# Value projections of the second mixer: from plain products to blocks of two column groups with sevens

## The chip, the cores and the metric

The kernel runs on one core of one Trainium2 chip. The metric is the device time of one launch in microseconds, as the median of several runs. TensorE multiplies matrices and writes into banks of accumulators, VectorE and ScalarE do elementwise work, SyncE (SP) issues the weight loads. Each engine works through its own queue in order and waits on semaphores for the others.

## The reference

Two layers over 256 positions of width 2048. Each layer adds a mixer and a gated feed-forward stage to the residual stream h. The first layer's mixer is a gated delta rule with a recurrent unit, the second layer's mixer is two kinds of attention, eight heads of 128 each; the change is in the second.

```python
def fox_moba_mixer(hn, w_in, f_bias, w_out):
    fq, fk, fv, ff, mq, mk, mv = split_cols(hn @ w_in, CD_SIZES)
    log_f = jax.nn.log_sigmoid(ff.astype(jnp.float32) + f_bias.astype(jnp.float32)).transpose(0, 2, 1)
    o_c = forgetting_attention(to_heads(fq, FOX_HEADS), to_heads(fk, FOX_HEADS), to_heads(fv, FOX_HEADS), log_f)
    o_d = moba_attention(partial_rotary(to_heads(mq, MOBA_HEADS)), partial_rotary(to_heads(mk, MOBA_HEADS)),
                         to_heads(mv, MOBA_HEADS))
    return jnp.concatenate([from_heads(o_c), from_heads(o_d)], axis=-1) @ w_out

def reference(x, ...):
...
    for layer in range(DEPTH):
        j = layer // 2
        if layer % 2 == 0:
            h = h + gdn_rglru_mixer(rmsnorm(h, ab_norm[j]), ...)
        else:
            h = h + fox_moba_mixer(rmsnorm(h, cd_norm[j]), cd_w_in[j], cd_f_bias[j], cd_w_out[j])
        h = h + swiglu(rmsnorm(h, ffn_norm[layer]), ffn_w_gate[layer], ffn_w_up[layer], ffn_w_down[layer])
    return rmsnorm(h, final_norm)
```

With 256 positions the second kind of attention (moba) has one block, so it is plain causal attention with a partial rotation. The values fv and mv are two products of 256 x 2048 by 2048 x 1024.

## The kernel before

**Precision.** Each matrix product is made of three matmuls of a reduced-precision format: an operand is split into a high part (a cast on ScalarE, L179) and a low part (the difference, on VectorE, L180); high x high, high x low and low x high are summed in one accumulator. The activations X are kept as high and low parts, tokens along the free dimension, 16 feature tiles of 128.

**Loads.** `load` (L166) fetches 512 KB of weights into one of three buffers `raw`; in the feed-forward stages some loads go to four further buffers, `raw4`. `split` makes `whi` (four buffers) and `wlo` (three). One load with its split is called a unit here.

**Products.** There are two ways to hold the operands. `wstat` (L187) keeps the weights stationary and makes queries and keys: 32 matmuls per 128 columns, with X's both parts moving. `xstat` (L280) keeps X stationary and streams weights of 512 columns: per unit two feature tiles, two halves of the tokens and three matmuls each, 12 matmuls of 512 columns; it uses two of the four large accumulators (`acc`). The values are made by `xstat`, one column group of 512 after the other, eight units each (`values`, L1033). The output projections use it too.

**Sevens.** The feed-forward stages use `block` (L409) instead. It makes two column groups and both token halves at once, in four accumulators F, and can do some feature groups (four feature tiles, 512 features) by seven products in place of eight, as Strassen and Winograd do with 2 x 2 blocks. The two operands' sums are made on VectorE: `combine` (L382) makes the four combinations of X of a feature group, `total` (L372) the four sums of weight blocks, each split again into a high part `thi` and a low part `tlo`. Four of the products go to four small accumulators M (the tag `ms`, four banks), three straight into F. When all sevens are done, `ends` (L449) makes from M the four corrections e0 to e3, and the caller adds each to, or subtracts it from, its F. `lead` and `trail` say how many plain units stand before and after the sevens.

**Order of the work.** Attention of each head is a generator (`attend`, L1042) with four steps. `tick` (L156), called after each unit, moves waiting generators on; the forgetting gate (`forget`, L1001) is one too. `need` runs generators until something is done, `finish` runs them all. So small matmuls of attention stand between the large ones of projections. They take their accumulators from the same four small banks. A scheduler of the language then fixes each engine's order of instructions from dependences and priorities; buffers of one tag rotate, and a new tile waits until the last reader of the buffer is done.

**The second mixer** (`mixer1`, L995): values of the first kind, the norm's reciprocal root (`rstd`, whose rows are then spread by `rstd_rows`), the forget gate, eight heads of queries and keys with their attention into `Of`; values of the second kind, eight heads with rotation and attention into `Om`; then the output projection over `Of` and over `Om`. `vv`, `Of` and `Om` are the three buffers of 16 KB per partition of the pool `og`.

Of the kernel before, what the change touches and what calls it, by code (L numbers as in the profile page):

```python
# [11 lines left out]
T = 256  # L12
# [35 lines left out]
def body(tc, A, out):  # L48
# [14 lines left out]
    loads, more = [0], []  # L63

    def phase(mixer):

        st = ExitStack()
        sub = lambda name, bufs: st.enter_context(tc.tile_pool(name=name, bufs=bufs))
        ogp.pool = sub("og" if mixer else "hid", 3 if mixer else 1)
        if not mixer:  # L70

            fp.pool = sub("fp", 1)
        mx.pool = sub("mx" if mixer else "fx", 1)
        more[:] = [] if mixer else [1]
        loads[0] = -12
        return st
# [265 lines left out]
    def rstd_rows():  # L342

        rs = nrm["rs"]
        dg = mx.tile([128, 2, 128], F32, name="dg", tag="t1", bufs=5)
# [36 lines left out]
    def combine(x4):  # L382

        f = mx.tile([128, 4, T], F32, name="cf", tag="T", bufs=3)
        c = mx.tile([128, 4, 2, 128], F32, name="cc4", tag="T", bufs=3)
        r = fp.tile([128, 2, 4, 2, 128], F32R, name="comb", tag="comb", bufs=3)
        V.tensor_tensor(out=f, in0=x4[:, :, 0].bitcast(F32), in1=x4[:, :, 1].bitcast(F32), op=ALU.add)
        a11, a21, a12, a22 = (f[:, 2 * j:2 * j + 2, t * 128:(t + 1) * 128] for j in range(2) for t in range(2))
        for i, (x, y) in enumerate(((a21, a22), (a21, a11), (a22, c[:, 1]), (a12, c[:, 2]))):
            V.tensor_tensor(out=c[:, i], in0=x, in1=y, op=ALU.subtract)  # L390
        S.copy(r[:, 0], c)
        V.tensor_tensor(out=r[:, 1], in0=c, in1=r[:, 0].bitcast(F32), op=ALU.subtract)
        return r
# [15 lines left out]
    def block(src, x, comb, nd, hooks, tail=0, lead=2, trail=None):  # L409
# [50 lines left out]
        for j, (i, u) in enumerate(plain):  # L460
# [91 lines left out]
    def small_proj(src, n):  # L552

        raw = mx.tile([128, NK, n], F32, name="sraw", tag="t1", bufs=5)
# [41 lines left out]
    def mixer0():  # L596
# [101 lines left out]
        def pair_task(pr):  # L698
# [8 lines left out]
            for j, hd in enumerate(hds):  # L707
                qk = qks[hd]
                sq = mx.tile([128, 2, 2, 128], F32, name="sq", tag="t2", bufs=4)
                vg = mx.tile([128, 2, 128], F32, name="vg", tag="t1", bufs=5)  # L710
# [11 lines left out]
                dec = mx.tile([128, 2, 128], F32, name="dec", tag="t1", bufs=5)  # L722
# [46 lines left out]
        def group_task(gr):  # L769
# [7 lines left out]
            Vc = mx.tile([128, 8, 32], F32, name="Vc", tag="t1", bufs=5)  # L777
# [36 lines left out]
            V1 = mx.tile([128, 8, 32], F32, name="V1", tag="t1", bufs=5)  # L814
# [11 lines left out]
            V1 = mx.tile([128, 8, 32], F32, name="V3", tag="t1", bufs=5)  # L826
# [146 lines left out]
        for n in range(8):  # L973
            lw = mx.tile([128, 2, 128], F32, name="lw", tag="t1", bufs=5)
# [20 lines left out]
    def mixer1():  # L995
# [35 lines left out]
        Om = ogp.tile([128, 8, 2, T], F32R, name="Om", tag="og")  # L1031

        def values(i):  # L1033
            for g in range(2):
                Ps = xstat(lambda k: X[:, k], [A["w1x"][2 * i + g, u] for u in range(8)])
                if i == g == 0:
                    rstd()
                    start(forget(), 1)
                for t in range(2):
                    V.tensor_scalar_mul(vv[:, i, t, g * 512:(g + 1) * 512], Ps[t], nrm["rs"][:, t:t + 1])  # L1040

        def attend(i, hd, q, k, O):  # L1042
            if i == 0:

                sel = mx.tile([40, 128], F32R, name="sel", tag="kt", bufs=HB)
# [38 lines left out]
        def qk_head(i, hd):  # L1084
            r = []
            for which in range(2):
                t = scaled(wstat(W[16 * i + 2 * hd + which], True), "qkt", SCALE if which == 0 else 1.0, "vt", HB)
                if i == 1:
                    sw = mx.tile([32, T], F32, name="sw", tag="t1", bufs=5)
# [20 lines left out]
        out_proj(lambda k: Om[:, k], lambda g: [wo[g, 4 + u] for u in range(4)], norm_then(cl["n3"]))  # L1110
# [166 lines left out]
```

## Time and profile before

| what | value |
|---|---|
| runs (3) | 2231.83, 2232.99, 2235.12 us; median 2232.99 |
| profiled execution, device time | 2232.51 us |
| its span in the profile | 2230.7 us |
| granted TensorE clock | 0.999 |
| TensorE busy | 2215.9 us, 99% |
| VectorE busy | 1928.9 us, 86% |
| ScalarE busy | 1278.9 us, 57% |

A page of the profile shows the busy time of each engine, the chain of work that ended last, and groups of instructions by source line with mean duration, idle time ahead and what ended it. PE is TensorE's matmuls, PEld its weight loads, DVE VectorE, ACT ScalarE, SPq the queue of SP. Names like `wlo<-raw,whi` are the program's tiles, output first. Busy time of TensorE overlaps from one matmul to the next; the distance between two starts is the price of one. The second mixer lies between 1128 and 1525 us of the span.

### The profile page before, as it was taken

The numbers are of one execution on the slowest core, as the hardware profiler recorded it, in microseconds if no ns is written. First come the engines' busy times: TensorE is split into PE (matmuls) and PEld (weight loads), VectorE is DVE, ScalarE is ACT, GpSimd is POOL, SyncE is SP. The second block draws the span as 40 slices with busy tenths as digits, with TensorE's granted clock in tenths as the row PEclk, the third lists the DMA queues.
The fourth block names the chain that finished last, engine by engine and source line by source line (L and its number), as shares of the span: only waits on it lengthen the run. The fifth ranks groups of instructions, "written<-read, shape, count | busy, mean of one in ns | idle before, by whom it ended". The sixth has DMA issues, their size and how long they took to land.

```text
span 2230.7 us, 30096 instructions
## 1 busy us (share of the span) xinstructions
PE 2215.9 (99%) x11026; PEld 1852.0 (83%) x11026; DVE 1928.9 (86%) x2716; ACT 1278.9 (57%) x1670; POOL 2.1 (0%) x6
## 2 busy tenths in 40 slices
PE   9999999999999999999999999999999999999998
PEld 8888888888888888888878888888888888888886
DVE  8899676789989999899966658857999999999998
ACT  6776664565555665565654444445665466555565
POOL 0000000000000000000000000000000000000000
PEclk9999999999999999999999999999999999999999
DMA  7445445665565666656545455456665666666563
GB/s 280 161 144 168 140 150 187 214 208 195 192 215 196 201 195 203 207 187 200 180 158 175 158 172 172 162 186 217 208 198 191 208 205 203 194 210 202 181 219 131
DMA packets 117780, 422.29 MB, mean 189 GB/s; under 512 B 13152, under 2 KB 14688, under 8 KB 117504
## 3 DMA queue, kind: packets, MB, share of 16 engines
q1 hardware_dynamic: 117344, 420.10, 56.7%
q8 instruction: 86, 1.41, 0.2%
q14 instruction: 62, 0.51, 0.1%
q10 hardware_dynamic: 288, 0.27, 0.0%
HBM read 418.22 MB, written 2.10 MB: 188 GB/s over the span
## 4 chain that ended last, share of the span: by engine, by line
PE 97%; DVE 1%; DMA 1%; ACT 0%; issue 0%; SPq 0%; DVEq 0%; ACTq 0%
PE F L405 16%; PE F L406 16%; PE F L404 16%; PE Pw L199 11%; PE Pw L204 6%; PE Px L303 5%; PE Px L305 5%; PE Px L304 5%; PE M L404 4%; PE M L405 4%; PE M L406 4%; PE Ph L492 1%; PE Psc L1053 1%; PE Pt L326 0%; PE Ps L563 0%; DMA raw<-in_gu 0%
## 5 line engine op out<-in xcount | busy, mean ns | idle before, releaser
L179 ACT CAST whi<-raw 128x1024 fp32r<-128x1024 f32 x724 | 760.7, 1052 | 744.8 <-PE F L406 359.1
L180 DVE TENSOR_TENSOR wlo<-raw,whi 128x1024 fp32r<-128x1024 f32 x724 | 876.5, 1219 | 185.0 <-PE Px L304 74.0
L199 PE MATMUL Pw<-X,whi 128*128 128x512 f32 x1088 | 388.0, 400 | 0.0
L404 PE MATMUL F<-whi,X 128*128 128x512 f32 x848 | 330.5, 391 | 0.0
L405 PE MATMUL F<-wlo,X 128*128 128x512 f32 x848 | 330.4, 390 | 0.0
L406 PE MATMUL F<-whi,X 128*128 128x512 f32 x848 | 330.1, 389 | 0.0
L204 PE MATMUL Pw<-X,wlo 128*128 128x256 f32 x1088 | 304.7, 280 | 0.1
L378 ACT CAST thi<-T 128x1024 fp32r<-128x1024 f32 x208 | 219.1, 1054 | 98.6 <-DVE T L375 71.5
L379 DVE TENSOR_TENSOR tlo<-T,thi 128x1024 fp32r<-128x1024 f32 x208 | 252.5, 1219 | 24.7 <-ACT thi L378 24.2
L199 PEld LDWEIGHTS Pw<-X,whi 128*128 128x128 f32 x1088 | 204.1, 188 | 47.4 <-issue 0.5
L405 PE MATMUL F<-wlo,hid 128*128 128x512 f32 x536 | 208.9, 390 | 0.0
L406 PE MATMUL F<-whi,hid 128*128 128x512 f32 x536 | 208.7, 389 | 0.0
L404 PE MATMUL F<-whi,hid 128*128 128x512 f32 x536 | 208.6, 390 | 0.0
L204 PEld LDWEIGHTS Pw<-X,wlo 128*128 128x128 f32 x1088 | 205.4, 189 | 1.2 <-DVE wlo L180 0.7
L406 PEld LDWEIGHTS F<-whi,X 128*128 128x128 f32 x848 | 159.2, 188 | 33.1
L404 PEld LDWEIGHTS F<-whi,X 128*128 128x128 f32 x848 | 159.2, 188 | 32.7
L405 PEld LDWEIGHTS F<-wlo,X 128*128 128x128 f32 x848 | 159.3, 188 | 32.5
L375 DVE TENSOR_TENSOR T<-raw,raw 128x1024 f32<-128x1024 f32 x98 | 119.2, 1218 | 11.0 <-DMA raw<-in_gu 8.9
L375 DVE TENSOR_TENSOR T<-T,raw 128x1024 f32<-128x1024 f32 x104 | 126.6, 1218 | 1.9 <-DMA raw<-in_dn 1.7
L404 PE MATMUL M<-thi,comb 128*128 128x512 f32 x312 | 121.3, 391 | 0.6 <-ACT thi L378 0.6
L405 PE MATMUL M<-tlo,comb 128*128 128x512 f32 x312 | 121.6, 390 | 0.0
L406 PE MATMUL M<-thi,comb 128*128 128x512 f32 x312 | 121.5, 389 | 0.0
(385 smaller groups left out, 3217.1 us busy)
## 6 DMA issues: line engine op xcount, KB each, us to landing
raw<-in_gu SPq DMA_DIRECT2D x352, 512.0 KB, 4.1
raw<-in_dn SPq DMA_DIRECT2D x176, 512.0 KB, 4.3
raw<-in_w0w SPq DMA_DIRECT2D x72, 512.0 KB, 3.6
raw<-in_wo SPq DMA_DIRECT2D x64, 512.0 KB, 3.5
raw<-in_w1w SPq DMA_DIRECT2D x64, 512.0 KB, 3.6
raw<-in_w1x SPq DMA_DIRECT2D x32, 512.0 KB, 3.6
raw<-in_w0x SPq DMA_DIRECT2D x16, 512.0 KB, 3.6
xw<-in_xw SPq DMA_DIRECT2D x6, 768.0 KB, 10.9
```

The costliest lines, as they stand in the source:

```text
L179: S.copy(hi, raw)
L180: V.tensor_sub(lo, raw, hi.bitcast(F32))
L199: PE.matmul(P.rearrange("p a b -> p (a b)"), hi[:, kk], X[:, k].rearrange("p a b -> p (a b)"), start=k == 0, stop=False)
L204: PE.matmul(P[:, 0], lo[:, kk], X[:, k, 0], start=False, stop=k == NK - 1)
L303: PE.matmul(Ps[t], x[:, 0, ts], hi[:, kk], start=k == 0, stop=False)
L304: PE.matmul(Ps[t], x[:, 0, ts], lo[:, kk], start=False, stop=False)
L375: V.tensor_tensor(out=t, in0=a, in1=b, op=ALU.add)
L378: S.copy(hi, t)
L379: V.tensor_sub(lo, t, hi.bitcast(F32))
L404: PE.matmul(self.t, xh, hi[:, kk], start=self.i == kk == 0, stop=False)
L405: PE.matmul(self.t, xh, lo[:, kk], start=False, stop=False)
L406: PE.matmul(self.t, xl, hi[:, kk], start=False, stop=kk == 1 and self.i == self.n - 1)
```

## The change

`values` uses `block`. The first value product does one of its four feature groups by sevens, with seven plain units ahead of them; the second does two. The combinations of X lie in `cmb`, which takes the third buffer of `og`; `Om` is made only after the second block and takes its place. The combination of the second feature group is made during the first kind of heads. While sevens are under way in the mixer, `tick` counts but moves no task (`paused`). The corrections are scaled on ScalarE by the norm's reciprocal root and joined with F on VectorE. Room for the new tiles comes from `t1` (four buffers in place of five in this mixer, `few`) and from `kt` (two in place of eight for `sel`); a fourth buffer for weight loads (`raw4`, one, each fourth load) is added, `extra`. `rstd` moves from behind the first column group to the block's ninth plain unit, the forget gate starts at the twelfth, and `need("forget")` stands after the first head's query and key.

```diff
@@ phase @@
-        if not mixer:
-
-            fp.pool = sub("fp", 1)
+
+        fp.pool = ogp.pool if mixer else sub("fp", 1)
...
-        loads[0] = -12
+        loads[0], extra[0] = -12, 0
@@ tick @@
         count[0] += 1
+        if paused[0]:
+            return
@@ load @@
             raw = mx.tile([128, 1024], F32, name="raw4", tag="raw4", bufs=4)
+        elif extra[0] and loads[0] % 4 == 3:
+            raw = mx.tile([128, 1024], F32, name="raw4", tag="raw4", bufs=1)
@@ combine @@
-    def combine(x4):
+    def combine(x4, r=None):
...
-        r = fp.tile([128, 2, 4, 2, 128], F32R, name="comb", tag="comb", bufs=3)
+        if r is None:
+            r = fp.tile([128, 2, 4, 2, 128], F32R, name="comb", tag="comb", bufs=3)
@@ block @@
                 if k == len(sevens):
                     e = ends()
+
+                paused[0] = not more and k < len(sevens)
@@ mixer1 @@
-        Om = ogp.tile([128, 8, 2, T], F32R, name="Om", tag="og")
+
+        cmb = ogp.tile([128, 2, 2, 4, 2, 128], F32R, name="cmb", tag="og")
+        cx = [None, None]
+
+        def combs(m):
+            cx[m] = combine(X[:, 4 * m:4 * m + 4], cmb[:, m])
 
         def values(i):
-            for g in range(2):
-                Ps = xstat(lambda k: X[:, k], [A["w1x"][2 * i + g, u] for u in range(8)])
-                if i == g == 0:
-                    rstd()
-                    start(forget(), 1)
-                for t in range(2):
-                    V.tensor_scalar_mul(vv[:, i, t, g * 512:(g + 1) * 512], Ps[t], nrm["rs"][:, t:t + 1])
+            hooks = ({5: lambda: combs(0), 8: rstd, 11: lambda: start(forget(), 1)}, {})[i]
+            F, e = block(lambda c, u: A["w1x"][2 * i + c, u], lambda k: X[:, k],
+                         {m: lambda m=m: cx[m] for m in range(1 + i)}, 4, hooks, lead=(7, 2)[i], trail=2)
+            rs = nrm["rs"]
+            for t in range(2):
+                for c in range(2):
+                    S.activation(e[t][c], e[t][c], AF.Copy, scale=rs[:, t:t + 1])
+                    V.scalar_tensor_tensor(out=vv[:, i, t, c * 512:(c + 1) * 512], in0=F[t][c], scalar=rs[:, t:t + 1], in1=e[t][c],
+                                           op0=ALU.mult, op1=ALU.subtract if t > c else ALU.add)
...
-                sel = mx.tile([40, 128], F32R, name="sel", tag="kt", bufs=HB)
+                sel = mx.tile([40, 128], F32R, name="sel", tag="kt", bufs=2)
...
+        extra[0], few[0] = 1, 4
         turns[0] = -1
-        for i, O in ((0, Of), (1, Om)):
+        for i in range(2):
             values(i)
+            O = Of if i == 0 else ogp.tile([128, 8, 2, T], F32R, name="Om", tag="og")
             if i == 0:
                 rstd_rows()
-                need("forget")
             for hd in range(NH):
                 q, k = qk_head(i, hd)
+                if i == hd == 0:
+                    need("forget")
+                if i == 0 and hd == 4:
+                    combs(1)
                 start(attend(i, hd, q, k, O), 4)
```

Elsewhere `bufs=5` of the tag `t1` becomes `bufs=few[0]`, which is 5 outside this mixer.

More of the change, by code (lines that the diff above doesn't have):

```diff
@@ L62, in body @@
     mx, ogp, fp = Phase(), Phase(), Phase()
-    loads, more = [0], []
+    loads, more, extra, paused, few = [0], [], [0], [0], [5]
     def phase(mixer):
@@ L344, in rstd_rows @@
         rs = nrm["rs"]
-        dg = mx.tile([128, 2, 128], F32, name="dg", tag="t1", bufs=5)
+        dg = mx.tile([128, 2, 128], F32, name="dg", tag="t1", bufs=few[0])
         P = ms([128, 2, 128], "Prb")
@@ L552, in small_proj @@
     def small_proj(src, n):
-        raw = mx.tile([128, NK, n], F32, name="sraw", tag="t1", bufs=5)
+        raw = mx.tile([128, NK, n], F32, name="sraw", tag="t1", bufs=few[0])
         nc.sync.dma_start(raw, src)
@@ L813, in group_task @@
                     PE.matmul(P1[s, m], Cb[s, m, s], Xi[s, m], start=True, stop=True)
-            V1 = mx.tile([128, 8, 32], F32, name="V1", tag="t1", bufs=5)
+            V1 = mx.tile([128, 8, 32], F32, name="V1", tag="t1", bufs=few[0])
             S.copy(V1, P1)
@@ L973, in mixer0 @@
         for n in range(8):
-            lw = mx.tile([128, 2, 128], F32, name="lw", tag="t1", bufs=5)
+            lw = mx.tile([128, 2, 128], F32, name="lw", tag="t1", bufs=few[0])
             nc.sync.dma_start(lw, A["lruw"][n])
@@ L1088, in qk_head @@
                 if i == 1:
-                    sw = mx.tile([32, T], F32, name="sw", tag="t1", bufs=5)
+                    sw = mx.tile([32, T], F32, name="sw", tag="t1", bufs=few[0])
                     V.stream_shuffle(sw, t[0:32], rot)
@@ L1109, in mixer1 @@
         turns[0] = 1
-        out_proj(lambda k: Om[:, k], lambda g: [wo[g, 4 + u] for u in range(4)], norm_then(cl["n3"]))
+        out_proj(lambda k: O[:, k], lambda g: [wo[g, 4 + u] for u in range(4)], norm_then(cl["n3"]))
     with phase(True):
```

8 lines of the change are left out of this document (4 added, 4 removed).

## The prediction

> **What bounds the kernel now.** I read the page first (busy shares, then the chain that ended last), then the waits of TensorE, then a table of windows by stage.
>
> ```profile
> span 2230.7 us, 30096 instructions
> PE 2215.9 (99%) x11026; PEld 1852.0 (83%) x11026; DVE 1928.9 (86%) x2716; ACT 1278.9 (57%) x1670; POOL 2.1 (0%) x6
> ...
> PE 97%; DVE 1%; DMA 1%; ACT 0%; issue 0%; SPq 0%; DVEq 0%; ACTq 0%
> ```
>
> TensorE is busy 99% of the span and holds 97% of the chain. Which stage has slack behind it is read from the windows; columns are the stretch, its length, then the busy time (and instructions) of each engine, the granted clock, the DMA share and GB/s.
>
> ```profile
> 470.00:1128.00 658.00, 657.60 (x2948) 543.54 (x2948) 627.70 (x651) 382.13 (x411) 0.00 (x0) 1.00 0.60 196
> 1128.00:1550.00 422.00, 422.00 (x2169) 355.14 (x2168) 291.52 (x549) 202.53 (x326) 0.00 (x0) 1.00 0.53 177
> 1335.00:1431.00 96.00, 96.00 (x555) 84.05 (x554) 82.80 (x189) 46.21 (x80) 0.00 (x0) 1.00 0.51 171
> ```
>
> The first row is the first feed-forward stage, which already uses the sevens: VectorE runs at 95% (627.70 of 658) and TensorE still never falls idle by more than 0.4 us. The second row is the second mixer, the only stage whose instructions the change touches: TensorE has no gap in 422 us, VectorE is at 69%. The third row is the part of the mixer with the second kind of query and key heads, where VectorE has 13.2 us free. So in the mixer time can only be won by fewer matmuls, and only be lost by making TensorE wait.
>
> **The price of a matmul.** Busy time per matmul (0.39) overlaps the next one, so the price is the distance between starts:
>
> ```profile
> 1142.44 0.39 PE L303 MATMUL Px<-whi,X 128*128 128x512 f32 x1
> 1142.67 0.39 PE L304 MATMUL Px<-wlo,X 128*128 128x512 f32 x1
> 1142.89 0.39 PE L305 MATMUL Px<-whi,X 128*128 128x512 f32 x1
> 1143.12 0.39 PE L303 MATMUL Px<-whi,X 128*128 128x512 f32 x1
> ```
>
> Three in 0.68 us: 0.227 us each. Before, each of the two value projections is 16 units (one load of 512 KB each) x 12 matmuls = 192. With sevens, a feature group costs 7 products x 6 = 42 instead of 4 units x 12 = 48. The first block has one such group (144 + 42 = 186), the second two (96 + 84 = 180): 6 + 12 = **18 matmuls fewer, 18 x 0.227 = 4.1 us less on TensorE**. In the built programs' order of instructions TensorE indeed has 18 fewer, and everything ahead of and behind the mixer stands as it stood. The weight loads of SP are as many; one buffer in four is now the extra one (raw4), four in rotation instead of three.
>
> **What it adds, on VectorE and ScalarE.**
>
> ```profile
> L180 DVE TENSOR_TENSOR wlo<-raw,whi 128x1024 fp32r<-128x1024 f32 x91 | 110.1, 1218 | 10.8 <-PE F L405 7.4 <-issue 2.6 <-ACT whi L179 0.7
> L379 DVE TENSOR_TENSOR tlo<-T,thi 128x1024 fp32r<-128x1024 f32 x35 | 42.5, 1219 | 5.3 <-ACT thi L378 5.2
> L453 DVE TENSOR_TENSOR e<-M,e 128x512 f32<-128x512 f32 x20 | 13.3, 684 | 0.4 <-PE M L406 0.4
> L522 DVE SCALAR_TENSOR_TENSOR fa<-e,rs,fa 128x512 f32<-128x512 f32 x6 | 4.4, 745 | 0.0
> L392 DVE TENSOR_TENSOR comb<-cc,comb 128x1024 fp32r<-128x1024 f32 x3 | 3.7, 1219 | 0.0
> L390 DVE TENSOR_TENSOR cc<-cf,cc 128x256 f32<-128x256 f32 x6 | 2.5, 418 | 0.0
> L387 DVE TENSOR_TENSOR cf<-X 128x1024 f32<-128x1024 f32 x1 | 1.2, 1211 | 0.0
> L391 ACT CAST comb<-cc x10: 1041/1054/1059, 443.5 to 2096.8; 128x1024 fp32r<-128x1024 f32 x10
> ```
>
> Per seven on VectorE: 3 splits and 4 totals of two instructions, 11 x 1.22 = 13.4 us, in place of 4 splits (4.9). Three sevens: +25.6 us. Two combinations: 2 x (1.21 + 4 x 0.42 + 1.22) = +8.2. Ends: 2 x 4 x 0.68 = +5.5. The outputs stay eight of 0.75. Together +39 us of VectorE in the mixer, 291.5 to about 331 of 418: 79%, under the 95% that the feed-forward stage bears. ScalarE gains 12 casts less 3, 2 combinations (1.05 each), 2 copies and 8 scalings of a half-size tile, under 20 us on 202 of 422. By totals all of it lies beside the matmuls. What counts is whether VectorE, one queue in order, delivers each low part in time.
>
> VectorE's own pace is better than its durations: independent neighbours start 1.14 us apart though each lasts 1.22.
>
> ```profile
> 1109.16 1.22 DVE L375 TENSOR_TENSOR T<-T,raw 128x1024 f32<-128x1024 f32 x1
> 1110.30 1.22 DVE L180 TENSOR_TENSOR wlo<-raw,whi 128x1024 fp32r<-128x1024 f32 x1
> ```
>
> I laid VectorE's instructions of both blocks in the built order at that pace against TensorE's at 0.227, by hand. Three places are tight.
>
> **(a) The third unit of the first block.** Its load goes to the raw4 buffer, so SP issues it behind the rope table, and that waits for the last sum of squares; in VectorE's order the first combination now stands ahead of this unit's low part.
>
> ```profile
> 1130.58 0.34 SPq L1028 DMA_DIRECT2D rope<-in_rope  x1
> 1130.97 0.41 SPq L555 DMA_DIRECT2D sraw<-in_w1s  x1
> ```
>
> ```profile
> 1129.11 0.47 PE L303 MATMUL Px<-whi,X 128*128 128x512 f32 x1
> ```
>
> ```profile
> 1129.49 1.26 DVE L328 SCALAR_TENSOR_TENSOR X<-Pt,col,X 128x256 fp32r<-128x256 f32 x3
> ...
> 1133.27 0.87 DVE L328 SCALAR_TENSOR_TENSOR X<-Pt,col,X 128x256 fp32r<-128x256 f32 x2
> 1134.06 1.21 DVE L180 TENSOR_TENSOR wlo<-raw,whi 128x1024 fp32r<-128x1024 f32 x1
> ```
>
> ```profile
> raw<-in_w1x SPq DMA_DIRECT2D x32, 512.0 KB, 3.6
> ```
>
> The load takes sraw's place at 1130.97, lands 3.6 later (1134.6), its cast ends at 1135.65 (1.05), when TensorE arrives there (about 1135.6: its first unit starts at 1129.11, with some 1.0 us of transposes among its matmuls, and two units of 12 x 0.227 follow). TensorE's order then has four matmuls with the high parts, until 1136.6. VectorE ends X at 1134.1 less the split that no longer stands between (1.14): 1132.95. Then the combination's sum 1.21, four differences and three tiny ones (some 2.0): 1136.2; the low part is there at 1137.4. TensorE **waits 0.8 us**. Bounds: 0, if the differences overlap fully; 2.0, if the load lands a microsecond late.
>
> **(b) The forget gate.** The first attention needs nf, whose cumulative sum (Pf) TensorE reaches behind a chain of tiny VectorE instructions. Before, that chain ran beside the second column group:
>
> ```profile
> 1165.06 0.36 DVE L575 TENSOR_SCALAR so<-Psq,rs 128x8 f32<-128x8 f32 x2
> ...
> 1175.93 0.25 DVE L1016 COPY lfw<-lf 128x16 f32<-128x16 f32 x2
> ...
> 1178.78 0.41 PE L1018 MATMUL Pf<-tab,lfw 128*40 128x128 f32 x2
> ```
>
> 11.1 us from so to lfw, with three splits between, and 2.6 us to spare before Pf. Now the projection starts only after the first block's last units, Psq follows the first query, and Pf stands two projections later: 64 matmuls (32 pairs, below) and one more: 32 x 0.353 + 0.24 = 11.5 us after its start, 11.7 with the gate's own small matmuls. In VectorE's order the last split before the chain's end waits until TensorE frees its buffer, half a projection (2.8) before Pf, and stands behind a query's add and scaling; counted from the second projection's start it begins near 9.3 and ends at 10.4; ten tiny instructions of 0.21 follow: 12.5, against 11.7 for Pf. **Wait 0.9 us**; bounds 0 and 2.6.
>
> ```profile
> 1209.93 0.40 PE L199 MATMUL Pw<-X,whi 128*128 128x512 f32 x1
> ...
> 1210.99 0.40 PE L199 MATMUL Pw<-X,whi 128*128 128x512 f32 x1
> ...
> 1169.89 0.18 DVE L120 TENSOR_SCALAR lf<-ls_z 128x16 f32<-128x16 f32 x1
> 1170.10 0.18 DVE L122 TENSOR_TENSOR lf<-lf,ls_z 128x16 f32<-128x16 f32 x1
> ```
>
> The first two rows are three pairs of a projection's matmuls apart: 1.06 / 3 = 0.353 us a pair. The last two give the chain's pace, 0.21.
>
> **(c) The second block.** Four accumulators are wanted at once, where the last two projections still hold two; the fourth waits for the add of the last key, behind T1, T3, two splits and a softmax on VectorE. Counted from the end of the last projection, VectorE gets the third split's buffer at 0 and ends it at 1.4, the first half of the softmax at 2.8, an attention output at 3.3 and the add at 3.9; TensorE, after 1.9 us of attention and one and a half units, wants the bank at 6.0: free. From there VectorE has T1's low part at 5.0, the softmax's end at 6.2, two splits and T3's low part at 9.5, T2 at 10.7, a split at 11.8, T4 at 12.9, T2's low part at 14.0, two splits at 16.3, the next T1 at 17.4 and T4's low part at 18.6. TensorE by then has done 1.9 + 3 units of 2.72 + 6 products of 1.36 = 18.3, and wants that low part 0.2 later: 18.5. Price **0.1**; bounds 0 and 2.2, the latter if 25 instructions each go 0.09 slower. The paused tasks hold two heads of softmax,
>
> ```profile
> 1203.00:1283.00 80.00, 2.46 (x15) 1.84 (x15) 10.13 (x36) 5.92 (x24) 1.00 0.48 162
> ```
>
> (the softmax tile alone, six heads: 1.7 us of VectorE each), which run in the block's last three units and the heads after, into the 13.2 us free there. The pause also keeps attention off the four small banks that the products fill. The output Om takes the combinations' place, whose last reader is the second block's last product, long before Om's first writer: nothing. Shorter rotations (t1, kt) make ScalarE wait for a first attention product once per head, where it is idle half the time: nothing.
>
> Sum: -4.1 + 0.8 + 0.9 + 0.1 = **-2.3 us**. The profiled execution took 2232.51 around its span of 2230.7; the median shown is 2232.99, half a microsecond above. 2230.2 from the one, 2230.7 from the other; I say 2230.3.
>
> **Rivals.**
> *All hidden.* No wait arises, as in the feed-forward stage, where 95% of VectorE leaves TensorE whole. For it: that row. Against: (a) and (b) are starts, not steady state. 2232.5 - 4.1 = 2228.4.
> *VectorE becomes the bound* (the other side). If its instructions went end to end at full duration, the first block would hold 15 splits, 8 of totals (28.1), 8.2 of combinations, 2.7 ends, 3.0 outputs, 2.8 of the norm, 3.4 of X: 48.2 against 186 x 0.227 + 0.9 = 43.1 of TensorE; the second 30 x 1.22 + 2.7 + 3.0 + 3.4 softmax + 2.5 = 48.2 against 180 x 0.227 + 3 = 43.9. Late by 5.1 and 4.3, less 4.1: +5.3, **2237.8**. It decides where the mean start distance on VectorE exceeds about 1.2 us. Against it: the 1.14 above, and three low parts held in advance. The Trainium skill states this case as a rule ("VectorE: DVE Perf Modes", the section on the DRAIN): the next vector instruction does not start until the previous has left the pipe; the same section lets one that is not held start earlier, and the trace agrees with that exception.
> *The backlog returns.* The held softmaxes and the longer first block push VectorE late into the second kind of heads, whose 13.2 us free are not where they are wanted; each of two heads then delays TensorE by one softmax (1.7): -2.3 + 3.4 = +1.1, 2233.6. Against: tasks wait for four ticks of 2.8 us anyway.
>
> **How the numbers follow.** Forecast 0.50, all hidden 0.28, VectorE the bound 0.10, backlog 0.12. Range 2228.0 to 2234.0: from all hidden less a little for the runs' own spread, to (a) to (c) near the middle of their upper bounds (6.8 together) and the backlog; what lies outside is the vector-bound case and some noise. About 0.2% (4.5 us) is what a measurement of this kernel tells from no change; the whole saving is 4.1, so faster by more than that needs the hidden case and a lucky median: 0.18. Slower by more is the vector-bound case and a corner of the backlog: 0.09. Within: 0.73.
>
> **What would show it.** In the profile after: 18 fewer matmuls; windows of the two blocks of about 43 and 44 us; TensorE's waits naming F L405 on a split of VectorE near 1137 (a), Pf on lfw near 1195 (b), and F L405 on tlo (c), each under 1 us. Many waits on tlo or wlo through both blocks, or M and F waiting for accumulators, would prove the vector-bound rival; none at all, the hidden one. I am wrong if the mixer is longer than before, or if the feed-forward stages change by more than 1 us.

## The result, and the profile after

The kernel after took **2230.17 us** (median of 22 runs, 2228.52 to 2233.31) against 2233.59 of the kernel before (22 runs beside it, 2231.34 to 2235.82). The ratio is 0.9984, with a 95% interval of 0.9978 to 0.9991: 2 to 5 us less. The forecast was 2230.3, in a range of 2228.0 to 2234.0. The interval holds the forecast's 2.3 us less and also the 4.1 of the rival without any wait, so the time alone does not tell these two apart.

A single execution's length is too coarse to check a sum of terms below one microsecond. In the 14 profiles of this study the first matmul of the value projections starts anywhere from 1127.94 to 1132.44 us after the span's start, ahead of everything that the change touches. So I read the mixer's own **stretch** in each trace: from that matmul to the first one of the output projection over Of. Taken twice for the kernel after it was 299.97 and 299.98. Here are the windows over exactly that stretch, first of the kernel before (stretch, its length, then busy time and instructions of PE, PEld, DVE, ACT, POOL):

```profile
1129.11:1431.50 302.39, 302.39 (x1616) 255.64 (x1614) 210.25 (x425) 141.90 (x236) 0.00 (x0) 1.00 0.51 169
```

and of the kernel after:

```profile
1129.80:1429.77 299.97, 298.83 (x1598) 252.15 (x1596) 242.98 (x466) 158.90 (x258) 0.00 (x0) 1.00 0.55 172
```

Eighteen matmuls fewer (1616 to 1598), 2.42 us less, and a TensorE that is no longer busy all the time (298.83 of 299.97). VectorE gained 32.7 us and ScalarE 17.0, and nearly all of it is invisible. The head of the page, and the windows of the first feed-forward stage, of the whole mixer, of the second kind of heads and of the mixer's two blocks:

```profile
span 2229.3 us, 30116 instructions
PE 2212.5 (99%) x11008; PEld 1848.8 (83%) x11008; DVE 1961.5 (88%) x2757; ACT 1295.3 (58%) x1691; POOL 2.1 (0%) x6
```

```profile
470.00:1128.00 658.00, 657.96 (x2950) 543.89 (x2949) 628.26 (x651) 381.57 (x409) 0.00 (x0) 1.00 0.62 196
1128.00:1550.00 422.00, 420.86 (x2161) 353.65 (x2160) 326.22 (x592) 221.06 (x351) 0.00 (x0) 1.00 0.56 179
1335.00:1431.00 96.00, 96.00 (x557) 84.14 (x556) 83.74 (x196) 47.16 (x85) 0.00 (x0) 1.00 0.53 169
1128.00:1176.00 48.00, 47.20 (x219) 38.52 (x218) 45.68 (x70) 31.77 (x46) 0.00 (x0) 1.00 0.62 200
1286.00:1330.00 44.00, 43.93 (x198) 35.89 (x197) 40.49 (x50) 26.22 (x35) 0.00 (x0) 1.00 0.59 185
```

The third row answers the backlog rival: through the heads of the second kind TensorE is busy 96.00 of 96.00. The fourth shows where most of the idle time is: 0.8 us in the first block.

The prediction named a change of the feed-forward stages by more than 1 us as a sign against itself. From the start of its first large matmul to that of its last the first of them took 697.13 us before, 696.73 after and 698.16 in the second profile of the kernel after; the second took 696.03, 696.95 and 696.42. But over the 14 profiles, in which no edit touches either stage, the first lies between 696.28 and 698.53 and the second between 695.07 and 697.21. So a limit of 1 us was too narrow for this sign, and nothing here stands out of that spread.

Three places lost time.

**(a)** TensorE's own timeline at the first block's third unit (start, duration, engine, line, operation; in brackets the idle time ahead of it and what ended it):

```profile
1135.91 0.39 PE L409 MATMUL F<-wlo,X 128*128 128x512 f32 x1
1136.14 0.39 PE L410 MATMUL F<-whi,X 128*128 128x512 f32 x1
1137.11 0.73 PE L408 MATMUL F<-whi,X 128*128 128x512 f32 x2 [0.59 <-ACT whi L182]
1138.06 0.73 PE L408 MATMUL F<-whi,X 128*128 128x512 f32 x2 [0.22 <-ACT whi L182]
```

Starts that should be 0.227 apart are 0.97 apart (1136.14 to 1137.11), then 0.34 and 0.61 (the grouped row hides the start at 1137.45), and 0.34 once more. Over the normal distance that is 1.35 us. The bracket names a **cast** on ScalarE, not a low part on VectorE. What the cast waited for stands in ScalarE's timeline, and what VectorE did meanwhile in its own:

```profile
1136.02 2.94 ACT L182 CAST whi<-raw 128x1024 fp32r<-128x1024 f32 x3 [2.60 <-DMA raw<-in_w1x]
```

```profile
1133.70 1.22 DVE L391 TENSOR_TENSOR cf<-X 128x1024 f32<-128x1024 f32 x1
...
1136.20 0.42 DVE L394 TENSOR_TENSOR cc<-cf,cc 128x256 f32<-128x256 f32 x1
1137.09 3.50 DVE L183 TENSOR_TENSOR wlo<-raw,whi 128x1024 fp32r<-128x1024 f32 x3 [0.47 <-ACT whi L182]
```

ScalarE stood idle 2.60 us until the load had landed. The combination's differences end at 1136.62; VectorE then waits 0.47 for the same cast before it makes the low part. The load was last, not the combination. The fourth unit's cast stands behind the third's on ScalarE, which is why the wait comes twice. The chain of waits in that window says the same in order of time (start, duration, what):

```profile
1130.52 0.73 ACT junk L320 x2
1131.24 0.37 ACT X L330
...
1131.66 4.33 DMA raw<-in_w1x
...
1136.02 0.02 ACT whi L182
```

The last sum of squares (junk) ends at 1131.25; then SP issues the rope table and behind it the load (SP's rows are below; the row of X is what ScalarE did meanwhile); then come 4.33 us of transfer and the cast. The page of this kernel gives a median of 4.3 us from issue to landing for the 32 loads of these weights (4.0 in its second profile), against 3.6 before. So this load was no slower than half of them; what sets it apart is that it was issued late.

Three more profiles have the same order of work up to here. In all four the load is issued 1.86 or 1.87 us after the first matmul, and the loss follows the transfer: 4.11 us of transfer and 1.14 us of loss (tot2x), 4.33 and 1.35 (after), 4.44 and 1.51 (after_again), 4.62 and 1.66 (nopause). So the size of (a) differs from run to run by up to half a microsecond.

**(b)** The forget gate, in the timelines of TensorE and of VectorE:

```profile
1196.73 0.39 PE L202 MATMUL Pw<-X,whi 128*128 128x512 f32 x1
1197.38 0.41 PE L1024 MATMUL Pf<-tab,lfw 128*40 128x128 f32 x2 [0.26 <-DVE lfw L1022]
```

```profile
1194.27 1.22 DVE L183 TENSOR_TENSOR wlo<-raw,whi 128x1024 fp32r<-128x1024 f32 x1
1195.41 0.17 DVE L121 TENSOR_TENSOR lf<-lf,ls_z 128x16 f32<-128x16 f32 x1
...
1197.08 0.25 DVE L1022 COPY lfw<-lf 128x16 f32<-128x16 f32 x2
```

0.65 us between starts, where the projection's own next matmul would come after 0.24. Not all of the difference is waiting: in pf_late, below, Pf waits for nothing and still starts 0.21 behind a matmul whose own successor would start after 0.12. Taking that 0.09 off leaves a wait of about 0.33 us. A split stands ahead of the chain's last tiny instructions, as forecast.

**(c)** In the second block the low part of a seven's last sum came late by 0.34 in this profile (0.46 and 0.34 between starts instead of 0.227 each), by 0.2 in the second profile of the same kernel:

```profile
1316.26 0.39 PE L408 MATMUL F<-thi,X 128*128 128x512 f32 x1
1316.72 0.50 PE L409 MATMUL F<-tlo,X 128*128 128x512 f32 x1
```

ScalarE's timeline shows a load ahead of it, once more, and VectorE's shows that the low part waited for a cast behind that load:

```profile
1312.45 2.01 ACT L182 CAST whi<-raw 128x1024 fp32r<-128x1024 f32 x2 [3.03 <-DMA raw<-in_w1x]
1314.36 1.04 ACT L381 CAST thi<-T 128x1024 fp32r<-128x1024 f32 x1
```

```profile
1315.44 1.23 DVE L382 TENSOR_TENSOR tlo<-T,thi 128x1024 fp32r<-128x1024 f32 x1 [0.68 <-ACT thi L381]
```

### The profile page after: what moved, and what is told of

It reads as the page before. It is cut to its first block, busy times and chain, and to the rows that moved or that the text cites. A ratio compares the mean times of both kernels' runs of the same rounds, so it can differ in the third digit from the quotient of the medians.

```text
span 2229.3 us, 30116 instructions
## 1 busy us (share of the span) xinstructions
PE 2212.5 (99%) x11008; PEld 1848.8 (83%) x11008; DVE 1961.5 (88%) x2757; ACT 1295.3 (58%) x1691; POOL 2.1 (0%) x6
## 4 chain that ended last, share of the span: by engine, by line
PE 95%; DVE 2%; DMA 1%; ACT 1%; issue 0%; DVEq 0%; ACTq 0%
PE F L409 17%; PE F L410 17%; PE F L408 17%; PE Pw L202 10%; PE Pw L207 5%; PE M L408 4%; PE M L410 4%; PE M L409 4%; PE Px L306 3%; PE Px L308 3%; PE Px L307 3%; PE Ph L498 1%; DVE wlo L183 1%; PE Psc L1066 1%; DMA raw<-in_w0w 1%; PE Pt L329 0%
## 5 line engine op out<-in xcount | busy, mean ns | idle before, releaser
L408 PE MATMUL F<-whi,X 128*128 128x512 f32 x934 | 364.3, 391 | 0.8 <-ACT whi L182 0.8
L409 PE MATMUL F<-wlo,X 128*128 128x512 f32 x934 | 364.1, 390 | 0.0
L410 PE MATMUL F<-whi,X 128*128 128x512 f32 x934 | 363.7, 389 | 0.0
L381 ACT CAST thi<-T 128x1024 fp32r<-128x1024 f32 x220 | 231.6, 1053 | 104.5 <-DVE T L378 74.7
L382 DVE TENSOR_TENSOR tlo<-T,thi 128x1024 fp32r<-128x1024 f32 x220 | 267.1, 1218 | 24.1 <-ACT thi L381 23.7
L408 PEld LDWEIGHTS F<-whi,X 128*128 128x128 f32 x934 | 175.2, 188 | 37.5 <-ACT whi L182 1.7
L410 PEld LDWEIGHTS F<-whi,X 128*128 128x128 f32 x934 | 175.3, 188 | 36.4
L409 PEld LDWEIGHTS F<-wlo,X 128*128 128x128 f32 x934 | 175.4, 188 | 35.7
L378 DVE TENSOR_TENSOR T<-T,raw 128x1024 f32<-128x1024 f32 x110 | 133.9, 1217 | 3.9 <-DMA raw<-in_dn 3.7
```

Source lines behind the costliest of these rows:

```text
L378: V.tensor_tensor(out=t, in0=a, in1=b, op=ALU.add)
L381: S.copy(hi, t)
L382: V.tensor_sub(lo, t, hi.bitcast(F32))
L408: PE.matmul(self.t, xh, hi[:, kk], start=self.i == kk == 0, stop=False)
L409: PE.matmul(self.t, xh, lo[:, kk], start=False, stop=False)
L410: PE.matmul(self.t, xl, hi[:, kk], start=False, stop=kk == 1 and self.i == self.n - 1)
```

## The experiments

Stretches below are split at the first matmul of the second block. They are worked out from starts of matmuls in each trace, like the distances named in the text. The first halves of the three kernels that were profiled twice repeat within 0.16 us. The second halves of the ten profiles whose second block is that of the kernel after lie between 144.58 and 145.25, so a gain of some tenths is read from the first half and not from the whole stretch. Kernels without a time have one timed run each, which tells nothing at this size.

| kernel (label) | to the second block | from it | stretch | time, median |
|---|---|---|---|---|
| before | 154.89 | 147.51 | 302.39 | 2233.59 |
| after | 155.08 | 144.89 | 299.97 | 2230.17 |
| after once more (after_again) | 155.24 | 144.74 | 299.98 | 2229.66 |
| before, 18 matmuls left out (price) | 153.56 | 144.79 | 298.34 | |
| raw4 late (a_load) | 155.32 | 144.77 | 300.09 | |
| rope table late (a_rope) | 155.86 | 144.68 | 300.54 | |
| raw4 from the seventh load (a_third, third_timed) | 154.03, 153.96 | 145.25, 144.58 | 299.27, 298.54 | 2229.01 |
| and gate two units earlier (both_9) | 154.58 | 144.97 | 299.56 | |
| and gate one unit earlier (both_10, both_10_timed) | 153.84, 153.99 | 145.02, 144.88 | 298.86, 298.88 | 2228.58 |
| no pause (nopause) | 155.35 | 144.87 | 300.23 | |
| sums made twice (tot2x) | 157.18 | 148.49 | 305.68 | |
| raw4 from the seventh load, Pf half a projection later (pf_late) | 153.41 | 144.85 | 298.26 | 2228.37 |

**The price of the matmuls alone.** In the kernel before:

```diff
-   PE.matmul(Ps[t], x[:, 0, ts], lo[:, kk], start=False, stop=False)
+   if not skip or not skip.pop(): PE.matmul(Ps[t], x[:, 0, ts], lo[:, kk], start=False, stop=False)
...
+   skip[:] = [1] * (3, 6)[i] + [0] * 24;
    Ps = xstat(lambda k: X[:, k], [A["w1x"][2 * i + g, u] for u in range(8)])
```

> The kernel before with 18 matmuls of its value projections left out (of the products with the low parts of the weights: 3, 3, 6 and 6 near the ends of the four projections), and nothing of the change. The mixer's stretch (first matmul of the value projections to the first of the output projection over Of) was 302.39 us in the profile of before. If a matmul's price is the 0.227 us between starts, as forecast: 18 x 0.227 = 4.1 less, 298.3. If the weights' loads, casts and splits set the pace there, none of it shows: 302.4.

298.34: 4.05 us less, split 1.33 and 2.72 between the halves (6 and 12 matmuls, 1.36 and 2.72 by the row's 0.227). The windows over its stretch show TensorE busy throughout:

```profile
1131.25:1429.59 298.34, 298.34 (x1598) 252.27 (x1595) 210.06 (x425) 141.99 (x236) 0.00 (x0) 1.00 0.57 171
```

So a removed matmul is worth its distance between starts here. The kernel after gets 2.42 of these 4.05. Against price its first half is 1.52 longer and its second 0.10: the loss is at the start of the mixer and at the gate, hardly in the second block. Against before, the first half is even 0.19 longer, though it has six matmuls fewer; the whole gain comes from the second (2.62).

**Place (a): the load or the combination?** Three kernels. The first, from the kernel after:

```diff
-        elif extra[0] and loads[0] % 4 == 3:
+        elif extra[0] and loads[0] > 0 and loads[0] % 4 == 3:
```

> The kernel after, but the extra buffer raw4 is used only from the mixer's fifteenth load on, so that the third unit's load goes to one of the three old buffers and isn't queued behind the rope table. The profile of after shows 1.35 us lost at the third and fourth unit. Theory of the late load: these 1.35 go, the mixer's stretch becomes 299.97 - 1.35 = 298.6 or up to 0.3 more. Theory of the prediction (the first combination stands ahead of the low part on VectorE): about 0.8 stays there, 299.4 or more. What can be given back: the buffers in the first block rotate by three, and a stall at the seven's loads would show as a wait on a cast.

The third load is issued 0.11 us before the first matmul here (1130.95), where raw4 had it 1.86 behind. The wait at the third unit is gone; no start there is more than 0.33 us behind the one before. The combination still stands ahead of low parts on VectorE, now those of the fifth and sixth units, and costs nothing. With the loss that follows the transfer, above, that settles (a): the late load. But the stretch is 300.09, outside both expected ranges, because the time is lost again at the seven's last sum:

```profile
1164.82 0.39 PE L408 MATMUL F<-thi,X 128*128 128x512 f32 x1
1166.56 0.50 PE L409 MATMUL F<-tlo,X 128*128 128x512 f32 x1 [1.35 <-DVE tlo L382]
```

Its VectorE timeline shows what is ahead of that low part:

```profile
1162.62 1.22 DVE L183 TENSOR_TENSOR wlo<-raw,whi 128x1024 fp32r<-128x1024 f32 x1
1163.75 0.48 DVE L351 TENSOR_SCALAR dg<-tab,rs 128x128 f32<-128x128 f32 x2
1164.14 1.22 DVE L391 TENSOR_TENSOR cf<-X 128x1024 f32<-128x1024 f32 x1
1165.28 1.22 DVE L382 TENSOR_TENSOR tlo<-T,thi 128x1024 fp32r<-128x1024 f32 x1
```

VectorE is late at the seven, and in its fixed order the sum of the second combination (cf), wanted only in the second block, stands ahead of the low part. (The text ahead of the prediction places this combination in the first kind of heads, where the program calls it; the traces have all of it in the first block. In the kernel after its last instruction starts at 1172.43.) A load is behind the lateness here too: ScalarE waited 1.91 us for one before its cast at 1158.12, and VectorE 0.93 for that cast. It is the stall at the seven's loads that the expectation named.

The next kernel keeps the extra buffer for the seven and takes only the third load from it:

```diff
-        elif extra[0] and loads[0] % 4 == 3:
+        elif extra[0] and loads[0] > -9 and loads[0] % 4 == 3:
```

> The kernel after, but the third load alone is taken from the extra buffer: raw4 is used from the seventh load on, so that the first block's seven keeps its four buffers (with raw4 held back to the fifteenth load, TensorE waited 1.51 us more than a matmul's 0.227 for the low part of the seven's last sum, and the mixer's stretch was 300.09). Theory of the late load, with room behind it: both waits are gone, the stretch is 299.97 - 1.35 = 298.6. Theory that VectorE gives no more: TensorE, 1.35 us earlier at the seven, waits there in its turn, and the stretch stays at 299.5 to 300.

299.27, between the two theories, and 298.54 when it was profiled again, 0.4 below the lower end that the last expectation of this section gives for it. The first half agrees in both (154.03, 153.96): 1.0 to 1.3 less than in the two profiles of the kernel after. The second half, which this edit leaves alone in the order of the work, came out 0.67 apart. Nearly all of the late load's 1.35 is won, and the first seven gives back about 0.2 (the distances at its last low part are 0.35 and 0.33 in one profile, 0.29 and 0.33 in the other; 0.227 is normal).

What made the load late? The prediction put it behind the rope table in SP's order:

```diff
-        nc.sync.dma_start(rope, A["rope"])
...
             if i == 0:
+                nc.sync.dma_start(rope, A["rope"])
                 rstd_rows()
```

> The kernel after with the rope table's load moved behind the first block, raw4 still used for the third load. If the third load is late because SP issues it behind the rope table (as the prediction said), the wait of 1.35 us goes, the stretch is 298.6. If it is late because raw4's own place is free only after the last sum of squares of the feed-forward stage, the load comes just the 0.39 us earlier that the table's issue took, and the wait shrinks from 1.35 to about 1.0: stretch 299.6.

SP's timeline of the kernel after, and of this one:

```profile
1131.27 0.34 SPq L1034 DMA_DIRECT2D rope<-in_rope  x1
1131.66 0.41 SPq L176 DMA_DIRECT2D raw<-in_w1x  x1
1132.13 0.42 SPq L561 DMA_DIRECT2D sraw<-in_w1s  x1
```

```profile
1131.61 0.33 SPq L176 DMA_DIRECT2D raw<-in_w1x  x1
1131.98 0.43 SPq L561 DMA_DIRECT2D sraw<-in_w1s  x1
1132.46 0.42 SPq L1116 DMA_DIRECT2D rope<-in_rope  x1
```

Counted from the first matmul (1129.80 and 1130.14) the load is issued at 1.86 and at 1.47: the 0.39 of the table's issue earlier and no more. So the table held it back for its own issue alone. What holds the load itself, now that no table is ahead of it, stands in the waits of SP's queue in this kernel:

```profile
SPq L176 <- ACT junk L320: 1.2, 1, 1.2
```

It is the last sum of squares of the feed-forward stage, whose memory raw4 takes over; the load is issued 0.02 us after it ends (1131.59). The times expected for both theories were missed all the same: the stretch is 300.54. The wait at the third unit was 1.63 instead of 1.0, because the transfer took 5.01 us: counted from the first matmul the load landed at 6.48, against 6.19 in the kernel after, and the wait is 0.28 longer. The first seven lost 0.41 more, at its last low part. Why the transfer took longer is open. The same place in SP's order has transfers of 4.11 to 4.98 in the other kernels made from the kernel after (tot2x and both_9 are the ends), so this run does not show that the table behind it slowed it down.

**Place (b): late start or place in the order?** On top of raw4 from the seventh load, the gate's start moved to another unit of the first block:

```diff
-            hooks = ({5: lambda: combs(0), 8: rstd, 11: lambda: start(forget(), 1)}, {})[i]
+            hooks = ({5: lambda: combs(0), 8: rstd, 9: lambda: start(forget(), 1)}, {})[i]
```

> The kernel with raw4 from the seventh load on, and the forget gate started two units earlier (at the first block's tenth unit instead of its last). Pf waited 0.43 us on lfw in the profile of after. If only the gate's late start makes that wait, it goes: stretch 298.6 - 0.4 = 298.2 where the third load's theory holds (299.5 where not). Rival: the gate's own small matmuls, now among the block's last units, wait for a small bank that the seven's results still hold, and TensorE loses 0.5 us or more there: 298.7 or more.

> As the kernel with the gate two units earlier, but one unit earlier (at the eleventh). The gate's chain has 2.7 us more before Pf than in the kernel after, against a wait of 0.43: the wait goes, stretch 298.2. Rival as there: a wait for a small bank, smaller by one unit (2.7 us), so none: then this one is the faster of the two.

Both missed. The wait did not go in either (both_9, then both_10):

```profile
1191.55 0.41 PE L1024 MATMUL Pf<-tab,lfw 128*40 128x128 f32 x2 [0.61 <-DVE lfw L1022]
```

```profile
1195.71 0.41 PE L1024 MATMUL Pf<-tab,lfw 128*40 128x128 f32 x2 [0.29 <-DVE lfw L1022]
```

In both_9 Pf starts 0.89 us behind a second matmul of a pair, where 0.21 is the distance without a wait; in both_10 0.69 behind a first one, where it would be 0.33. That is 0.68 and 0.36 too late. No matmul of the gate waited for a small bank, so the rival given for both_9 fell as well, although its stretch is as long as that rival said: 0.53 us of it was lost at the last low part of the first seven, where both_10 lost nothing. When the chain moves forward, TensorE's order puts Pf forward with it, and it waits there again. Hence the next kernel leaves the chain where it was and moves only Pf:

```diff
             yield
-            yield
-            yield
-            yield
             V.memset(lw, 0.0)
             for c in (0, 32):
                 V.tensor_copy(lw[:, :, c:c + 8], lf)
+            while "go" not in done:
+                yield
             Pf = ms([40, 2, 128], "Pf")
...
+                if i == 0 and hd == which == 1: done.add("go")
                 t = scaled(wstat(W[16 * i + 2 * hd + which], True), "qkt", ...
...
-                if i == hd == 0:
-                    need("forget")
```

> The kernel with raw4 from the seventh load on, and the gate's cumulative sum Pf half a projection (8 pairs of matmuls, 2.8 us) later in TensorE's order, its chain on VectorE unmoved. With the gate started one and two units earlier Pf moved forward with its chain and waited as before (0.43 to 0.66 us more than a matmul's distance), so the theory is that the place of Pf against the end of its chain makes the wait, not the late start: now Pf waits for nothing, and the mixer's stretch is 0.4 less than 298.54 and 299.27 (two profiles of the kernel with Pf in the old place): 298.1 to 298.9. Rival: the first attention product, which needs Pf's result and now stands 2.8 us nearer behind it, waits in its place, and nothing is won: 298.5 to 299.3 with a wait of 0.4 there.

298.26. TensorE's and VectorE's timelines of this kernel:

```profile
1196.16 0.28 PE L207 MATMUL Pw<-X,wlo 128*128 128x256 f32 x1
1196.37 0.41 PE L1023 MATMUL Pf<-tab,lfw 128*40 128x128 f32 x2
```

```profile
1193.80 0.25 DVE L1019 COPY lfw<-lf 128x16 f32<-128x16 f32 x2
```

Pf follows at once, 2.3 us behind the end of its operand, and the first attention product waits for nothing either; the table of TensorE's waits has no row at all over the stretch. What made (b) is the distance in TensorE's order between Pf and the end of its chain. With (a) and (b) both removed the stretch is that of price within 0.1 us: the time lost in the first half is accounted for. (The two waits were 1.68 in the kernel after, and its first half 1.52 longer than price's: some 0.16 was regained at places that were not traced.) Not all of the 0.55 to 0.62 by which the first half is shorter than that of raw4 from the seventh load is Pf, though. Pf's wait is 0.33 of it; the other 0.2 is the first seven's last low part, which is in time here and was late in both profiles of that kernel. The edit was not aimed at it, and a single profile does not show whether it would come again. TensorE's busy time over it:

```profile
1127.94:1426.20 298.26, 298.21 (x1597) 252.32 (x1596) 242.19 (x466) 157.64 (x257) 0.00 (x0) 1.00 0.53 173
```

**Is VectorE near its limit?** In the kernel after, each sum of a seven written twice:

```diff
-        V.tensor_tensor(out=t, in0=a, in1=b, op=ALU.add)
+        for _ in range(1 if more else 2): V.tensor_tensor(out=t, in0=a, in1=b, op=ALU.add)
```

> The kernel after with every sum of the sevens in the mixer made twice on VectorE: 4 instructions more in the first block and 8 in the second, 12 of about 1.14 us from start to start, the same values. If VectorE were the bound of the blocks, all of it would come to the mixer's stretch: 299.97 + 13.7 = 313.7. If it has the slack that the totals say (some 5 us in the first block, 6 in the second), the first block grows by under 1 and the second by 1 to 4: 301 to 305. If there is slack to spare, under 301.

305.68: 5.7 us longer, 2.1 in the first half and 3.6 in the second, a little over my range of 301 to 305. Of 13.7 us of added work 8.0 stayed hidden, so VectorE does not bound the unmodified blocks; but 2.1 of the first half's 4.6 showing means that less than 3 us of room is left there. The waits are the vector-bound rival's, named in the table of TensorE's waits of this kernel (what was waited for; us in total, times, longest):

```profile
PE M L408 <- ACT thi L381: 1.2, 2, 0.6
PE F L409 <- DVE wlo L183: 1.0, 1, 1.0
PE M L409 <- DVE tlo L382: 0.8, 1, 0.8
PE Pf L1024 <- DVE lfw L1022: 0.6, 1, 0.6
PE F L408 <- ACT whi L182: 0.6, 2, 0.4
```

In the kernel after the same table, over the whole mixer, has two rows, and neither names a low part (the delay of (c) shows in distances between starts alone, since busy times of matmuls overlap):

```profile
PE F L408 <- ACT whi L182: 0.8, 2, 0.6
PE Pf L1024 <- DVE lfw L1022: 0.3, 1, 0.3
```

**Is the pause worth anything?**

```diff
-                paused[0] = not more and k < len(sevens)
+                paused[0] = 0
```

> The kernel after with the tasks not paused while sevens are under way: attention products of the first kind of heads then stand among the sevens of the second block. If the pause matters, they wait for the four small banks that the sevens' products fill, and TensorE, in order, waits with them: 2 us or more on the mixer's stretch (302 or more). If it doesn't matter, 299.97 within 0.5.

300.23, 0.26 more than after, of which 0.27 lies before the second block, where the order of the work is the same (the wait at (a) was 1.66 in this execution). The attention products move from the heads into the block, and nothing waits for them. The pause neither costs nor wins here.

**Timed side by side.** The unchanged kernel after and two versions, with five rounds each:

> The kernel after, unchanged, timed beside the next two on one chip. Its mixer was 2.42 us shorter than before in the two profiles: 0.9989 of the time before. Measured so far: 0.9984, interval 0.9978 to 0.9991. If the mixer is all of it, 0.9989 stays in the new interval; a stretch of 299.5 to 300.5.

> The kernel with raw4 from the seventh load on and the gate one unit earlier, whose mixer took 298.86 us in one look: 3.53 less than before, 1.11 less than after. If that is steady, 0.9984 of the time before and 0.9995 of the kernel after, whose difference of 1.1 us lies about within what the intervals can tell; stretch within 0.4 of 298.9. If the one look was luck, the stretch is 299.3 to 300.

> The kernel with raw4 from the seventh load on alone: 299.27 us in one look, 0.70 less than after. If steady, stretch within 0.4 of 299.3 and a time between the two others.

Ratios to the kernel before: after 0.9984 (0.9976 to 0.9993), gate one unit earlier 0.9982 (0.9973 to 0.9991), raw4 from the seventh load 0.9978 (0.9969 to 0.9987); pf_late, timed by itself, 0.9982 (0.9973 to 0.9991). All are faster than before, and none can be told from another. The stretches separate pf_late from the kernel after by 1.7 us. The medians go the same way without proving it: pf_late is 4.3 us below the kernel before that was timed beside it, the kernel after 3.4 and 3.6.

## Why the prediction was right, point by point

- **The bound.** TensorE's starts set the time, 0.227 us a matmul. Right: price gives 4.05 against 4.1.
- **VectorE and ScalarE beside the matmuls.** +39 us and under +20 forecast. VectorE's durations, added up over the stretch, grew by 38.9; busy time, which counts overlapping instructions once, by 32.7, and ScalarE's by 17.0. Hidden as forecast, but with little room in the first block (tot2x). The sentence that 79% of the mixer is under the 95% that the feed-forward stage bears was a poor guide: in the first block's window it is 45.68 of 48.00, which is that 95%.
- **(a), 0.8 with bounds 0 and 2.0.** Right place, wrong reason, a term too small: 1.35. Two of its sentences failed. "The load ... lands 3.6 later" took the median of the kernel before; with the change the median itself is 4.0 to 4.3, and this load took 4.36 from issue to cast. That alone made the load last and the combination harmless. And "SP issues it behind the rope table" was true but worth 0.39 us alone, since a_rope showed that the load waits for raw4's own place. The upper bound, "if the load lands a microsecond late", described what happened.
- **(b), 0.9 with bounds 0 and 2.6.** Mechanism right (a split ahead of the tiny chain), size about 0.33. The forecast had Pf wanted 11.7 us after the second projection's start and its operand there at 12.5. Counted from that start (1185.31) it was wanted at 11.7 and there at 12.0 (1197.33): the half microsecond too much is in VectorE's chain. What I counted as the cause, that the projection starts later, is not one: both_9 and both_10.
- **(c), 0.1.** 0.10 against price over the whole half, 0.2 to 0.34 at the place itself. (The forecast's own figures, 1.9 and twice 8.16, make 18.2 and not 18.3, and so a price of 0.2.) But it came on the second seven, not the first, and behind a load (ScalarE idle 3.03 us until it) rather than behind VectorE's queue. What this half regained elsewhere, some 0.25, was not traced.
- **Om in the combinations' place, shorter rotations: nothing.** No wait names them.
- **The sum.** -2.3 forecast, -2.42 measured between profiles. The three terms were 1.8 together and 1.63 net of the 4.05, with errors of +0.55, -0.57 and about nothing that nearly cancel: that the sum fits so closely is luck, the more so as (a) alone ranged from 1.14 to 1.66. So is the time: 2230.3 was counted from 2232.5 to 2233.0, and the kernel before took 2233.59 beside the kernel after. The difference of the times (3.4) is larger than the stretch's, and its interval holds both.
- **The rivals.** All hidden (2228.4): not what happened, but what pf_late reaches in the stretch, by the buffer's and Pf's place (and a first seven that lost nothing there); its median was 2228.37. VectorE the bound: refuted in the unmodified kernel, 8.0 of 13.7 us still hidden when work was added. In tot2x, VectorE's timeline has instructions of 1.22 us start 1.14 apart. The rule of the Trainium skill ("VectorE: DVE Perf Modes", "The DRAIN you can't avoid") would have had them end to end; the trace again agrees with that section's exception, by which an instruction that is not held starts earlier:

```profile
1151.61 1.22 DVE L378 TENSOR_TENSOR T<-raw 128x1024 f32<-128x1024 f32 x1
1152.74 1.22 DVE L183 TENSOR_TENSOR wlo<-raw,whi 128x1024 fp32r<-128x1024 f32 x1
```

- **The backlog.** Refuted: no idle time in the heads of the second kind.

## What to carry to other kernels

When matmuls are removed from a stage that TensorE bounds, the saving is their number times the distance between starts, less what is late at the stage's **first** units and at one-off chains; steady state hid 33 us of VectorE here and the start lost 1.14 to 1.66. A buffer that takes over memory of the stage before was filled here only after that stage's last reader was done, so give such a buffer to a later load, not to one of the first three. Where a wait stays after its chain was started earlier, look at where the waiting instruction stands in its own engine's order and move that instead.

## What the runs showed that I had not expected

The loads of these weights took longer with the change: a median of 4.3 and 4.0 us from issue to landing on the two pages of the kernel after, 3.6 before. Why was not tried. The one that counted took 4.11 to 4.62 in four runs of one order, and TensorE's loss followed it. The mixer's stretch repeated within 0.02 us in two of three kernels that were profiled twice (299.97 and 299.98, 298.86 and 298.88) while their starts in the span lay over a microsecond apart (1129.80 and 1131.03, 1130.86 and 1132.06); the third differed by 0.73, nearly all of it in the second half. For edits worth a microsecond the stretch of a trace decided earlier here than 11 timed runs.
